# Convolution sums in PSUM, and the seven half products of a group continued in three PSUM banks

## The chip, the cores and the metric

The kernel runs on one core of one Trainium2 chip. The metric is device time in microseconds (us) of one execution; lower is better. "PE" is the tensor engine, "DVE" the vector engine, "ACT" the scalar engine, "POOL" GpSimd and "SP" the queue that issues most transfers. PSUM is the tensor engine's output memory: eight banks of 512 float32 values in each of 128 partitions.

## What is computed

Three blocks, one after the other, on 1024 tokens of 1024 channels in float32. The parts that the change touches are a gated feed-forward network in the first block, the input product, gates, rotary turn and depthwise convolution of the second, and the input product of the third. Cut to that:

```python
# block 1
u_, g_ = (rmsnorm(x) @ ffn_w_in).split                       # 1024 -> 2 x 2816
x = x + (silu(g_) * u_) @ ffn_w_out
# block 2
a, b, cg, q, k, v, gate = (modulated_norm(x) @ w_in_2).split # 1024 -> several x 1024
y = a * sigmoid(b)
y = causal_depthwise_conv(y, conv_w_2, conv_b_2)             # 31 taps per channel
y = silu(layernorm(y)) ...                                   # then a product, times silu(cg)
r = retention(rotary(q), rotary(k), v, silu(gate))           # 4 heads of 256, in chunks of 128 tokens
# block 3
u_s5, z_s5, z_ssd, xBC, dt = (rmsnorm(x) @ w_in_3).split     # 1024 -> ...
```

## The kernel before

Every product of float32 operands is made of three matmuls per tile of weights: both operands are split into a high and a low part (the high part by ACT at L151, the low part by DVE or POOL at L152), and high times high, high times low and low times high are summed in PSUM (L625 to L627 in the class `Mixed`, L226 to L228 elsewhere).

The class `Mixed` (L554 to L672) computes two tiles of 128 outputs for all 1024 tokens, four halves of 128 x 512, with seven products of half matrices in place of eight. One such set is called a group here. A product is 12 matmuls of 128 x 512 (four tiles of weights, three matmuls each), so a group is 84. The parts of the weights are sums and differences of quarters of the weight matrix, made by POOL in place (L597, L599, L602, L605) in the raw tiles that SP loads (L584). The products are run in the order of `ORDER` (L566): a11, a12, s2, s3, s1, s4, a22. Each one goes to a PSUM bank of its own (`WITH`, L568: three banks "mm", two "pa", two "pb"; an eighth, "pc", is for small things), and `gather` (L631) takes it from there: ACT copies a11 (L639), and DVE makes seven additions of 128 x 512, each of a tile in SBUF and the bank (L636), of which s1 needs two. In SBUF the partial sums are carried from one half of the outputs to the next.

`Mixed` is used in four places:

- the feed-forward network's input (`FFN.products`, L728): 22 groups. When a group is complete DVE multiplies both of its output tiles with the row factors (L744, L746), ACT applies Silu, POOL multiplies the two (L747). The low parts of the weights are split by DVE.
- its output (L867 to L900): 8 groups, where ACT, DVE and POOL add the products to the residual `h`; POOL adds what lies in a tile `v` (L865).
- the input of block 2 (`block2`, L1151 to L1246): 24 groups in the order of `plan`: two gates, two convolution pairs, then six times one convolution pair and two of the groups q, k and v, and two gates at the end. Here the low parts are split by POOL (`on_pool`, L1222), except in the first two groups. For q and k, DVE and POOL turn the result (L1201 to L1206: four multiplications by DVE and two additions by POOL for each half of the tokens). For a convolution pair, DVE writes a * sigmoid(b) to the tile `A[c]` (L1192), and 32 steps for its 31 taps are put on a list of background work.
- the input of block 3 (`block3`): 12 groups, behind which POOL runs a scan.

The first two groups of each use are interleaved by `early` (L654), since their second factors come late.

The convolution (`tap`, L1139): per tile of 128 channels one DVE instruction for the first tap (L1143) and 30 for the others (L1147): `acc = A[:, j:j+1024] * w_j + acc`, with 128 x 1024 elements. `acc` lies in SBUF. The last tap writes to `A[c]`. There are eight such tiles, so 8 first taps and 240 others. They are paced by the tensor engine's products: each product of four tiles of weights adds `rate` x 4/16 steps (`worked`, L231), with the rate RT = 6.5, or RQ = 5.5 in the groups q and k; each step may start only behind the last DVE addition of the products (`core.paced`, L1172, used in `tick`, L157). What is left of the taps when the groups are through is run in the next stage, the retention (L1248 to L1428), whose background work at the rate RB is otherwise the layer norm of the convolution (`ln_sum` to `ln_scale`): it needs all taps.

A scheduler orders the instructions of each engine when the kernel is built; on the chip each engine runs its own list strictly in order, and waits where an operand or a place is not ready.

Of the kernel before, what the change touches and what calls it, by code (L numbers as in the profile page):

```python
# [32 lines left out]
RQ = 5.5  # L33
RT = 6.5
# [23 lines left out]
class Core:  # L58
    """Constants, shared pools and the dense products that every part uses."""

    def __init__(self, ctx, tc, ins):
# [11 lines left out]
        self.ps = ctx.enter_context(tc.tile_pool(name="psum", bufs=1, space=PSUM))  # L73
        self.dr = ctx.enter_context(tc.tile_pool(name="dram", bufs=1, space=DRAM))
# [54 lines left out]
    def load_blocks(self, eng, b0, b1):  # L129
        """Blocks of 128 of those vectors."""  # L130
# [41 lines left out]
    def behind(self, steps):  # L172
        """Steps that are to run behind the coming products, whose results wait for them."""
# [6 lines left out]
    def result(self, evac):  # L180
        """A product is emitted: evac() takes it from PSUM, once no step is left."""
# [7 lines left out]
    def norm_steps(self, acc, pool, to, **kw):  # L189
        """Steps to to["rbc"] = rsqrt of the token means of acc, over partitions."""  # L190
# [13 lines left out]
    def weights(self, w, row0, nk, col0, ncol=P, order=lambda t: t, into=None):  # L204
        """Columns col0.. of rows row0.. of w as [128, nk, ncol] parts; order(t) views the parts' columns as w's."""
# [12 lines left out]
    def mm3(self, ps, wts, xs, half, k0=0, start=True, stop=True, ncol=P):  # L218
        """ps[ncol, 512] += weights.T @ x over the k tiles of xs (each [128, 2, 1024])."""
# [11 lines left out]
    def worked(self, n):  # L231
        """Products with n tiles of weights are emitted: a share of the other work may follow."""
# [26 lines left out]
    def rows(self, r, pool):  # L259
        """[128 tokens, n] in two parts"""  # L260
# [6 lines left out]
    def spread_halves(self, rt, tag="pc"):  # L267
        """Parts of [128 tokens, 8] -> for each half, [128, 512] in PSUM, the same in every partition."""
# [9 lines left out]
    def over_partitions(self, rt, pool, tag="rbc", bufs=1, out=None, psum="pc"):  # L278
        """Parts of [128 tokens, 8] -> [128, 1024], the same in every partition."""
# [6 lines left out]
    def square_sum(self, acc, src, sl, first, pool, gain=None, bufs=2):  # L286
        """acc[:, sl] += (src * gain)^2"""
# [9 lines left out]
    def small_transposed(self, src, PT):  # L297
        """Tokens-major DRAM [1024, 256] -> two channel tiles, split."""
# [15 lines left out]
def attention(core, X, scratch):  # L314
    """Stick-breaking attention of every head, its output split in place of X; p @ ple_w_proj goes to DRAM meanwhile."""
# [7 lines left out]
    with ExitStack() as st:  # L323
# [63 lines left out]
        def projections():  # L387
            """Every pair's q, k and v, a few products at a time."""
# [16 lines left out]
            # X is free now  # L405
# [35 lines left out]
        def fill(n, limit):  # L441
            """Emit n (on average) of the products' pieces, but none of the pair after the next."""
# [232 lines left out]
def halves(t):  # L675
    return t[:, hs(0)], t[:, hs(1)]
# [1931 lines left out]
```

## Time and profile before

| what | value |
|---|---|
| median of 3 runs | 3820.76 us (3819.53 to 3821.97) |
| span of the profiled execution | 3820.3 us |
| PE busy | 3470.7 us (91%) |
| DVE busy | 2853.5 us (75%) |
| POOL busy | 1981.7 us (52%) |
| ACT busy | 1479.0 us (39%) |
| taps L1147 into `cacc` | 232, 425.3 us, mean 1833 ns |

The profile is of one execution. "Busy" is the time in which an engine has an instruction in work; matmuls overlap, so a busy PE need not be at its peak. A share over the whole span is an average over stages that are limited by different things, so the rows below are mostly of single stretches of time. Line numbers (L1147) are those of the kernel before. [...]

### The profile page before, as it was taken

The page shows a single profiled execution, that of the slowest core. Times are in us where ns is not written, and L with a number is a line of the kernel's source. Part 1 is how long each engine was busy: PE and PEld are TensorE (multiplying, and loading weights), DVE is VectorE, ACT ScalarE, POOL GpSimd, SP SyncE. Part 2 cuts the span into 40 slices and gives each one's busy share as a digit, 9 for nine tenths or more (in the row PEclk, how much of TensorE's full clock was granted, in tenths as well). Part 3 has the DMA queues.
Part 4 walks back from the last instruction along what each step waited for, and adds up shares of the span by engine and source line. Part 5 has one row for each costly group of instructions (what it writes and reads, how often), then busy time and mean ns, then how long its engine had stood idle before and what let it go on. Part 6 is the DMA issues. An engine that isn't in the chain of part 4 may idle for free. (4 is left out here: it accounts for less than half of the span.)

```text
span 3820.3 us, 45970 instructions
## 1 busy us (share of the span) xinstructions
PE 3470.7 (91%) x16540; PEld 2789.2 (73%) x16540; DVE 2853.5 (75%) x3453; ACT 1479.0 (39%) x2551; POOL 1981.7 (52%) x1690
## 2 busy tenths in 40 slices
PE   8999999999999999877878898989999679899998
PEld 7878777777787787755656677768778468677776
DVE  7888897888878646699999997784768455655644
ACT  5666683422234345311212224223432113753334
POOL 2333342566655434788898744244518874331122
PEclk9999999999999999999989999999999889899999
DMA  4111026333336324212211344466453125225513
GB/s 140 37 35 31 27 83 235 98 111 113 103 104 199 97 90 139 72 50 72 61 64 53 111 143 133 114 196 194 144 155 111 57 75 157 87 75 177 193 48 113
DMA packets 431134, 409.85 MB, mean 107 GB/s; under 512 B 34059, under 2 KB 364347, under 8 KB 430907
## 3 DMA queue, kind: packets, MB, share of 16 engines
q1 hardware_dynamic: 396164, 330.27, 27.8%
q0 software_dynamic: 21088, 68.19, 4.9%
q10 hardware_dynamic: 13655, 8.46, 0.8%
q8 instruction: 131, 2.15, 0.2%
q14 instruction: 96, 0.79, 0.1%
HBM read 284.80 MB, written 122.03 MB: 106 GB/s over the span
## 5 line engine op out<-in xcount | busy, mean ns | idle before, releaser
L151 ACT ACTIVATE whi<-raw 128x512 fp32r<-128x512 f32 (+3 forms) x610 | 431.3, 736 | 1105.7 <-POOL raw L599 234.1
L152 DVE TENSOR_TENSOR wlo<-raw,whi 128x512 fp32r<-128x512 f32 (+3 forms) x456 | 517.7, 1154 | 136.4 <-ACT whi L151 134.1
L226 PE MATMUL mm<-x,whi 128*128 128x512 f32 x1152 | 462.2, 402 | 6.1 <-DVE h L830 2.8
L227 PE MATMUL mm<-x,whi 128*128 128x512 f32 x1152 | 460.5, 400 | 3.5 <-DVE x L152 3.3
L228 PE MATMUL mm<-x,wlo 128*128 128x512 f32 x1152 | 458.7, 399 | 3.2 <-DVE wlo L152 3.2
L1147 DVE SCALAR_TENSOR_TENSOR cacc<-cv,par,cacc 128x1024 f32<-128x1024 f32 x232 | 425.3, 1833 | 2.5
L485 POOL TENSOR_TENSOR s<-s,f 128x127 f32<-128x127 f32 (+1 forms) x192 | 194.0, 1018 | 293.3 <-DVE f L484 189.2
L152 POOL TENSOR_TENSOR wlo<-raw,whi 128x512 fp32r<-128x512 f32 x154 | 296.0, 1941 | 14.9 <-ACT whi L151 14.9
L226 PE MATMUL mm<-yc,whi 128*128 128x512 f32 (+1 forms) x656 | 268.1, 409 | 32.9 <-ACT yc L151 28.2
L227 PE MATMUL mm<-yc,whi 128*128 128x512 f32 (+1 forms) x656 | 267.9, 408 | 4.4 <-DVE yc L152 4.3
L228 PE MATMUL mm<-yc,wlo 128*128 128x512 f32 (+1 forms) x656 | 264.7, 405 | 0.1
L226 PEld LDWEIGHTS mm<-x,whi 128*128 128x128 f32 x1152 | 219.4, 191 | 53.3 <-DVE h L830 3.5
L228 PEld LDWEIGHTS mm<-x,wlo 128*128 128x128 f32 x1152 | 219.3, 190 | 50.1 <-DVE wlo L152 4.7
L227 PEld LDWEIGHTS mm<-x,whi 128*128 128x128 f32 x1152 | 219.6, 191 | 48.8 <-DVE x L152 4.0
L484 DVE TENSOR_TENSOR_SCAN f<-f 128x128 f32<-128x128 f32 (+1 forms) x192 | 195.9, 1034 | 40.2 <-ACT f L477 39.0
L627 PE MATMUL mm<-x,wlo 128*128 128x512 f32 x456 | 186.3, 409 | 30.4 <-POOL wlo L152 17.1
L597 POOL TENSOR_TENSOR raw<-raw 128x512 f32<-128x512 f32 x58 | 91.3, 1574 | 221.6 <-DMA raw<-in_w_in_dram 80.4
L625 PE MATMUL mm<-x,whi 128*128 128x512 f32 x456 | 184.7, 405 | 5.2 <-ACT whi L151 3.8
L627 PE MATMUL pb<-x,wlo 128*128 128x512 f32 x432 | 176.5, 409 | 13.0 <-POOL wlo L152 9.9
L626 PE MATMUL mm<-x,whi 128*128 128x512 f32 x456 | 184.6, 405 | 3.6 <-DVE x L152 3.6
L626 PE MATMUL pb<-x,whi 128*128 128x512 f32 x432 | 174.8, 405 | 4.7 <-DVE x L152 4.7
L625 PE MATMUL pb<-x,whi 128*128 128x512 f32 x432 | 175.7, 407 | 3.5 <-DVE g L636 3.5
(618 smaller groups left out, 9092.4 us busy)
## 6 DMA issues: line engine op xcount, KB each, us to landing
raw<-in_w_in_dram SPq DMA_DIRECT2D x96, 512.0 KB
raw<-in_ffn_w_in_dram SPq DMA_DIRECT2D x44, 512.0 KB
raw<-in_w_out_dram SPq DMA_DIRECT2D x32, 512.0 KB
g<-g_dram SPq DMA_DIRECT2D x56, 256.0 KB
raw<-in_sb_w_in_dram SPq DMA_DIRECT2D x24, 512.0 KB
raw<-in_ada_w_dram SPq DMA_DIRECT2D x24, 512.0 KB
raw<-h_dram SPq DMA_DIRECT2D x18, 512.0 KB
g_dram<-t POOLq DMA_DIRECT2D x8, 1024.0 KB, 5.2
```

What stands on the lines that cost most here:

```text
L151: nc.scalar.activation(hi, src, AF.Copy)
L152: return (eng or nc.vector).tensor_tensor(lo, src, hi.bitcast(F32), ALU.subtract).ins
L226: nc.tensor.matmul(ps, w_h, x[:, 0, sl], start=start and k == 0, stop=False)
L227: nc.tensor.matmul(ps, w_h, x[:, 1, sl], start=False, stop=False)
L228: self.last = nc.tensor.matmul(ps, w_l, x[:, 0, sl], start=False, stop=stop and k == n - 1).ins
L484: nc.vector.tensor_tensor_scan(rev, rev, rev, 1.0, ALU.mult, ALU.bypass)
L485: nc.gpsimd.tensor_tensor(s[:, :m - 1], s[:, :m - 1], f[:, 1:m], ALU.mult)
L597: self.eng.tensor_tensor(at["s1"], at["a21"], at["a22"], ALU.add)
L625: nc.tensor.matmul(ps, hi[:, i], x[i][:, 0], start=i == 0, stop=False)
L626: nc.tensor.matmul(ps, hi[:, i], x[i][:, 1], start=False, stop=False)
L627: self.core.last = nc.tensor.matmul(ps, lo[:, i], x[i][:, 0], start=False, stop=i == self.N - 1).ins
L1147: nc.vector.scalar_tensor_tensor(out, A[c][:, j:j + S], core.vec("conv_w_2", j * KT + c), state["acc"], ALU.mult, ALU.add)
```

## The change

Two things are changed, and the pacing is fitted to them.

1. The convolution's running sum `acc` is a PSUM tile of two banks instead of an SBUF tile. The three banks "mm" are given back for the time of block 2's groups (`core.banks`), and taken again after it. The taps' rates are RT = 8 and RQ = 6, and what is left of the taps is run before the stage ends.
2. The products of a group go to three banks, a, b and c, and continue there: bank a takes a11, then s2, then s3, then a22 on top of each other; bank b takes a12; bank c takes s1, then s4. Between them ACT copies the partial sum out (after a11, s2 and s1), and DVE adds the bank to a tile three times (after a12, s3 and s4). The last value of bank a is taken by ACT (with the gate's or the convolution's function, where there is one) or, in the feed-forward network, by a DVE multiplication with the row factors. The order is a11, a12, s2, s1, s3, s4, a22. So a group has 3 DVE additions for 7, and 3 copies by ACT, and a fourth at its end in blocks 2 and 3, for 1.

The diff, cut to its core:

```diff
-RQ = 5.5
-RT = 6.5
+RQ = 6
+RT = 8
...
+        self.lent = ctx.enter_context(ExitStack())
+        self.banks()
...
+    def banks(self, name="psum_mm"):
+        self.lent.close()
+        self.psm = self.lent.enter_context(self.tc.tile_pool(name=name, bufs=1, space=PSUM))
+
     def psum(self, tag, shape=(P, HALF)):
-        bufs = {"mm": 3, "pa": 2, "pb": 2, "pc": 1}[tag]
-        return self.ps.tile(list(shape), F32, tag=tag, name=self.nm(tag), bufs=bufs)
+        pool, bufs = {"mm": (self.psm, 3), "acc": (self.psm, 1), "pa": (self.ps, 2), "pb": (self.ps, 2), "pc": (self.ps, 1)}[tag]
+        return pool.tile(list(shape), F32, tag=tag, name=self.nm(tag), bufs=bufs)
...
 class Mixed:
-    ORDER = ("a11", "a12", "s2", "s3", "s1", "s4", "a22")
-    WITH = {"a11": ("11", "mm"), "a12": ("21", "pb"), "s2": ("t2", "pa"), "s3": ("t3", "mm"), "s1": ("t1", "pb"),
-            "s4": ("22", "pa"), "a22": ("t4", "mm")}
+    ORDER = ("a11", "a12", "s2", "s1", "s3", "s4", "a22")
+    WITH = {"a11": ("11", "a"), "a12": ("21", "b"), "s2": ("t2", "a"), "s1": ("t1", "c"), "s3": ("t3", "a"),
+            "s4": ("22", "c"), "a22": ("t4", "a")}
+    TAGS = {"a": "pb", "b": "pa", "c": "pa"}
...
     def product(self, grp, name, x):
-        which, tag = self.WITH[name]
-        ps, x = self.core.psum(tag), x[which]
+        which, bank = self.WITH[name]
+        x, first = x[which], name in ("a11", "a12", "s1")
+        if first:
+            grp["ps"][bank] = self.core.psum(self.TAGS[bank])
+        ps, more = grp["ps"][bank], not first
         for i in range(self.N):
-            nc.tensor.matmul(ps, hi[:, i], x[i][:, 0], start=i == 0, stop=False)
+            nc.tensor.matmul(ps, hi[:, i], x[i][:, 0], start=first and i == 0, stop=False, skip_group_check=more)
...
-    def gather(self, name, ps, y):
+    def gather(self, name, ps, y, last):
         if name == "a11":
+            nc.scalar.activation(g1, ps, AF.Copy)
+        elif name == "a12":
+            add(g1)
+        elif name == "s2":
             nc.scalar.activation(g2, ps, AF.Copy)
-        elif name == "a12":
-            add(g1, g2)
-        elif name == "s2":
-            add(g2, g2)
+        elif name == "s1":
+            nc.scalar.activation(u2, ps, AF.Copy)
         elif name == "s3":
-            add(u1, g2)
-        elif name == "s1":
-            add(u2, u1)
-            add(g2, g2)
+            add(u2)
         elif name == "s4":
-            add(g2, g2)
+            add(g2)
         else:
-            add(u1, u1)
+            last(u1, ps)
...
     def early(self, product, gather, step=lambda: None):
         both(0, "a11", "a12")
         step()
-        product(0, "s1")
+        both(0, "s1")
         product(0, "s4")
         step()
         both(1, "a11", "a12")
         step()
         both(0, "s2", "s3")
-        gather(0, "s1")
         gather(0, "s4")
         both(0, "a22")
-        both(1, "s2", "s3", "s1", "s4", "a22")
+        both(1, *self.ORDER[2:])
...
 (FFN.products)
+            def scaled(u1, ps):
+                nc.vector.tensor_tensor(u1, ps, norm["rbc"][:, hs(0)], ALU.mult)
...
-                nc.vector.tensor_tensor(u, u, rbc, ALU.mult)
+                nc.vector.tensor_tensor(u[:, hs(1)], u[:, hs(1)], rbc[:, hs(1)], ALU.mult)
...
 (the FFN's output in block1)
+                        out = {"a11": g1, "a12": g1, "s2": g2, "s1": u2, "s3": u2, "s4": g2, "a22": u1}[name]
+                        if name in ("a11", "s2", "s3"):
+                            v = gp.tile([P, HALF], F32, tag="v", name=core.nm("v"), bufs=2)
                             nc.scalar.activation(v, ps, AF.Copy)
+                            add(out, v, nc.gpsimd)
                         elif name == "s1":
+                            v = gp.tile([P, HALF], F32, tag="v", name=core.nm("v"), bufs=2)
+                            nc.scalar.activation(v, ps, AF.Copy)
+                            add(out, v, nc.gpsimd)
                         else:
-                            add(u1, ps)
+                            add(out, ps)
...
 (block2)
-                    state["acc"] = cvp.tile([P, S], F32, tag="cacc", name=core.nm("cacc"))
+                    state["acc"] = core.psum("acc", (P, S))
...
         core.rate = RT
+        core.banks("psum_conv")
...
+                of = {"gate": AF.Silu, "conv": AF.Sigmoid}.get(kind, AF.Copy)
+                           lambda u1, ps: nc.scalar.activation(u1, ps, of))
-                if name != "a11":
+                if name in ("a12", "s3", "s4"):
                     core.paced = mix.last
...
-                if name in ("a11", "a12", "s2", "s3"):
+                if name in ("a11", "a12", "s1", "s2", "s3"):
                     gather(f, name)
...
             while turns:
                 turns.pop(0)()
+            core.paced = None
+            core.drain()
         scratch["mixed"].close()
+        core.banks()
```

The last group of block 2 (L1231) keeps its order a11, a12, s1, s4, s2, s3, a22. In block 3 the last value of bank a is copied by ACT. Comments and docstrings were taken out as well.

## Rows read from the trace of the kernel before

**Rows 1.** The page, busy time of each engine over the whole span.
```profile
PE 3470.7 (91%) x16540; PEld 2789.2 (73%) x16540; DVE 2853.5 (75%) x3453; ACT 1479.0 (39%) x2551; POOL 1981.7 (52%) x1690
```
**Rows 2.** Busy us and instructions per engine by stretch, then clock, DMA share, GB/s.
```profile
700.00:1160.00 460.00, 443.62 (x1911) 357.13 (x1909) 386.57 (x401) 151.07 (x242) 284.34 (x186) 0.99 0.32 103
1160.00:1335.00 175.00, 166.77 (x706) 133.57 (x706) 130.59 (x166) 66.18 (x113) 92.50 (x63) 0.98 0.45 145
1600.00:2187.00 587.00, 475.50 (x1853) 360.34 (x1852) 578.58 (x434) 118.75 (x197) 512.57 (x261) 0.92 0.21 64
2187.00:2395.00 208.00, 185.11 (x927) 155.52 (x926) 173.24 (x245) 79.91 (x122) 96.10 (x90) 0.96 0.45 142
2700.00:2975.00 275.00, 266.37 (x1313) 211.55 (x1312) 208.46 (x247) 95.80 (x138) 146.16 (x199) 0.98 0.41 130
```
**Rows 3.** What PE waited for in 1600 to 2187: total us, times, longest.
```profile
PE mm L627 <- POOL wlo L152: 48.1, 27, 5.8
PE pa L627 <- POOL wlo L152: 23.4, 13, 4.2
PE pa L625 <- ACT whi L151: 13.2, 5, 6.0
```
**Rows 4.** Instructions of single lines, whole span: ns min/median/max, first to last start.
```profile
L1147 DVE SCALAR_TENSOR_TENSOR cacc<-cv,par,cacc x232: 1249/1720/3467, 1601.5 to 2278.2; 128x1024 f32<-128x1024 f32 x116
L636 DVE TENSOR_TENSOR g<-g,pb x116: 671/675/707, 729.3 to 2969.8; 128x512 f32<-128x512 f32 x116
L1205 DVE TENSOR_TENSOR u<-u,cos x16: 680/1771/1784, 1676.0 to 2109.6; 128x512 f32<-128x512 f32 x16
L152 DVE TENSOR_TENSOR x<-h,x x16: 675/678/1780, 1505.8 to 1541.4; 128x512 fp32r<-128x512 f32 x16
L152 POOL TENSOR_TENSOR wlo<-raw,whi x154: 1269/2244/2283, 1569.9 to 2163.2; 128x512 fp32r<-128x512 f32 x154
L639 ACT ACTIVATE g<-mm x58: 576/582/677, 727.5 to 2960.3; 128x512 f32<-128x512 f32 x58
```
**Rows 5.** DVE in order of time (start, us), while POOL computes nothing.
```profile
2205.81 5.24 DVE L1147 SCALAR_TENSOR_TENSOR cacc<-cv,par,cacc 128x1024 f32<-128x1024 f32 x4
```
**Rows 6.** Groups of DVE instructions in 1600 to 2187: busy us, mean ns, idle before.
```profile
L1147 DVE SCALAR_TENSOR_TENSOR cacc<-cv,par,cacc 128x1024 f32<-128x1024 f32 x190 | 362.8, 1910 | 2.1
L636 DVE TENSOR_TENSOR g<-g,pb 128x512 f32<-128x512 f32 x42 | 28.2, 674 | 0.6 <-ACT g L639 0.6
...
L1205 DVE TENSOR_TENSOR u<-u,cos 128x512 f32<-128x512 f32 x16 | 26.7, 1667 | 0.0
...
L1201 DVE TENSOR_TENSOR rt<-g,sin 128x512 f32<-128x512 f32 x16 | 22.7, 1418 | 3.6 <-POOL g L1204 3.6
...
L1192 DVE TENSOR_TENSOR cv<-g,u 128x1024 f32<-128x1024 f32 x7 | 13.4, 1915 | 0.0
...
L1143 DVE TENSOR_SCALAR cacc<-cv,par 128x1024 f32<-128x1024 f32 x7 | 8.1, 1164 | 0.1
```
**Rows 7.** PE in order of time (start, us) in block 2's groups, undisturbed.
```profile
1657.16 0.39 PE L627 MATMUL mm<-t,wlo 128*128 128x512 f32 x1
...
1658.56 0.39 PE L627 MATMUL mm<-t,wlo 128*128 128x512 f32 x1
```
**Rows 8.** Groups of POOL instructions in 1600 to 2187.
```profile
L152 POOL TENSOR_TENSOR wlo<-raw,whi 128x512 fp32r<-128x512 f32 x144 | 283.3, 1986 | 7.1 <-ACT whi L151 7.1
...
L597 POOL TENSOR_TENSOR raw<-raw 128x512 f32<-128x512 f32 x20 | 34.8, 1741 | 38.1 <-DMA raw<-in_w_in_dram 33.6 <-PE pa L626 4.5
```
**Rows 9.** Taps in 2190 to 2450: a group of DVE instructions.
```profile
L1147 DVE SCALAR_TENSOR_TENSOR cacc<-cv,par,cacc 128x1024 f32<-128x1024 f32 x42 | 62.5, 1489 | 0.4
```
**Rows 10.** What PE waited for in 2187 to 2395, the retention.
```profile
PE pc L1376 <- DVE rstate L1385: 10.7, 2, 9.6
```
**Rows 11.** What PE waited for in 700 to 1160, the feed-forward network's input.
```profile
PE mm L627 <- DVE wlo L152: 5.9, 5, 1.9
...
PE mm L625 <- ACT g L639: 1.0, 1, 1.0
```

More of the change, by code (lines that the diff above doesn't have):

```diff
@@ L575, in group @@
     def group(self, w, row0, ca, cb, order=lambda t: t):
-        return {"src": (w, row0, ca, cb), "raw": {}, "ready": {}, "order": order}
+        return {"src": (w, row0, ca, cb), "raw": {}, "ready": {}, "order": order, "ps": {}}
     def load(self, grp, which):
@@ L621, in product, with add @@
         hi, lo = grp["ready"].get(name) or self.part(grp, name)
-        which, tag = self.WITH[name]
-        ps, x = self.core.psum(tag), x[which]
+        which, bank = self.WITH[name]
[3 more added lines that the diff above has]
+        ps, more = grp["ps"][bank], not first
         for i in range(self.N):
-            nc.tensor.matmul(ps, hi[:, i], x[i][:, 0], start=i == 0, stop=False)
-            nc.tensor.matmul(ps, hi[:, i], x[i][:, 1], start=False, stop=False)
-            self.core.last = nc.tensor.matmul(ps, lo[:, i], x[i][:, 0], start=False, stop=i == self.N - 1).ins
+            nc.tensor.matmul(ps, hi[:, i], x[i][:, 0], start=first and i == 0, stop=False, skip_group_check=more)
+            nc.tensor.matmul(ps, hi[:, i], x[i][:, 1], start=False, stop=False, skip_group_check=more)
+            self.core.last = nc.tensor.matmul(ps, lo[:, i], x[i][:, 0], start=False, stop=i == self.N - 1, skip_group_check=more).ins
         self.core.worked(self.N)
         return ps
-    def gather(self, name, ps, y):
+    def gather(self, name, ps, y, last):
         nc = self.core.nc
         (g1, g2), (u1, u2) = y
-        def add(out, a):
-            self.last = nc.vector.tensor_tensor(out, a, ps, ALU.add).ins
+        def add(out):
+            self.last = nc.vector.tensor_tensor(out, out, ps, ALU.add).ins
         if name == "a11":
+            nc.scalar.activation(g1, ps, AF.Copy)
+        elif name == "a12":
+            add(g1)
+        elif name == "s2":
             nc.scalar.activation(g2, ps, AF.Copy)
-        elif name == "a12":
-            add(g1, g2)
-        elif name == "s2":
-            add(g2, g2)
+        elif name == "s1":
+            nc.scalar.activation(u2, ps, AF.Copy)
         elif name == "s3":
-            add(u1, g2)
-        elif name == "s1":
-            add(u2, u1)
-            add(g2, g2)
+            add(u2)
         elif name == "s4":
-            add(g2, g2)
+            add(g2)
         else:
-            add(u1, u1)
+            last(u1, ps)
     def early(self, product, gather, step=lambda: None):
@@ L847, in block1 @@
             x11, x21, t1, x22 = (ffn.x[n] for n in ("11", "21", "t1", "22"))
-            places = [(y3, x11, x21, y0, y1, t1, x22), (y2, y3, x11, x21, y0, y1, t1)]
+            places = [(y3, x11, x21, y0, t1, y1, x22), (y2, y3, x11, x21, y0, t1, y1)]
             def second(chunk, name, pool):
@@ L1183, in gather, with gate @@
                         turns.pop(0)()
-            def gate(i, k, y):
-                nc.scalar.activation(y, y, AF.Silu)
+            def gate(i, k, y, rest):
+                nc.scalar.activation(y[:, rest], y[:, rest], AF.Silu)
                 nc.sync.dma_start(heads["gate"][i, :, k], y)
@@ L1190, in conv @@
                 nc.vector.memset(A[c][:, :PAD], 0.0)
-                nc.scalar.activation(b, b, AF.Sigmoid)
+                nc.scalar.activation(b[:, hs(1)], b[:, hs(1)], AF.Sigmoid)
                 nc.vector.tensor_tensor(A[c][:, PAD:], a, b, ALU.mult)
@@ L1242, in block2 @@
                         core.split(t1[:, 0], t1[:, 1], a)
-            for name in ("s1", "s4", "a22"):
+            for name in ("s4", "a22"):
                 gather(f, name)
@@ L1921, in gather @@
                 at[f, "g"] = gp.tile([P, S], F32, tag="g", name=core.nm("g"), bufs=2)
-            if name == "s3":
+            if name == "s1":
                 at[f, "u"] = gp.tile([P, S], F32, tag="u", name=core.nm("u"))
             g, u = at[f, "g"], at.get((f, "u"))
-            mix.gather(name, at[f, name], (halves(g), halves(u) if u is not None else (None, None)))
+            mix.gather(name, at[f, name], (halves(g), halves(u) if u is not None else (None, None)),
+                       lambda u1, ps: nc.scalar.activation(u1, ps, AF.Copy))
             out, m = (u_out, 2 * f) if f < 4 else (z_out, 2 * (f - 4))
```

28 lines of the change are left out of this document (6 added, 22 removed).

## The prediction

> **What bounds the kernel now.** I read the busy times over the whole span first [rows 1]: PE 91%, which says "tensor bound" and hides that the stages differ. So next the busy times by stage [rows 2]. In the feed-forward network's input and output (700 to 1335) and in block 3's groups (2700 to 2975) PE is busy 96, 95 and 97%: what they could gain is at most their idle 16 + 8 + 9 us. In block 2's groups, from the first tap to the last product (1600 to 2187, 587 us), it is another engine: DVE is busy 578.6 of 587 us, POOL 513, PE only 476, at a granted clock of 0.92. Then the waits there [rows 3]: PE waits for POOL's low parts of the weights. So DVE and POOL are both full, and the reader should ask whether they fill each other.
>
> They do [rows 4, 5]. Four taps with no POOL instruction beside them take 5.24 us, 1.31 each; in the stage the mean is 1.91 [rows 6]. A rotary multiplication of 512 elements takes 0.68 us at best and 1.77 in the median; POOL's split 1.27 at best, 2.24 in the median. Both grow by about 1 us, the length of the other's instruction: of DVE's instructions with two tile inputs in SBUF and POOL's, one waits for the other. The additions L636, with one input in SBUF and one in PSUM, run in the same minutes and took 671 to 707 ns in all 116 cases: they never wait. So a tap with its sum in PSUM, which reads one tile from SBUF, should drop out of this contest.
>
> **The change part by part.**
>
> *The taps.* In the stretch there are 196 taps now (190, and 6 that write the tile `cv`) at 1.91 us, 374 us. The counts of steps: the list gets 8 x 32 = 256; with rates 8 and 6 a product adds 2 or 1.5 steps, so a group of seven 14 or 10.5. From the fourth group on that is 13 x 14 + 8 x 10.5 = 266, and adding up group by group the list never runs dry before the last group and is empty by that group's second product. So all 240 taps come into this stage, and nothing is left to the drain. One costs 1.31 (the undisturbed row). No row shows DVE writing to PSUM: from below I take 1.25, the shortest tap, from above 1.91, today's mean, and choose 1.31, since the addition that reads PSUM costs the same 675 ns as a split between SBUF tiles [rows 4]. 240 x 1.31 = 314, so 60 us less for 44 taps more. The 8 first taps go from 1.16 to perhaps 1.3 each: 2 us more.
>
> [...]
>
> *The additions.* Per group 7 become 3. The stretch has 21 groups: 147 - 63 = 84 additions x 0.674 = 57 us less DVE. ACT gets 3 more copies of 0.58 us per group [rows 4], 37 us on top of 119 of 587: it lies beside. If ACT were held up by a split that waits for POOL, it would not; that is rival C.
>
> *The rotary multiplications.* 64 at a mean of 1.50 (the two rows stand for four), 96 us. POOL is left with the same 261 instructions, but with 1.27 instead of 1.97 us for most; their chance to meet falls. Bounds 0.68 and 1.50; I take 1.3: 13 us less. The seven products a * sigmoid(b) (1.9 us [rows 6]), also with two inputs in SBUF, are left as they are.
>
> *Sum for the stage.* DVE 578.6 - 60 + 2 - 57 - 13 = 451 us. What is late next: PE, at 1853 matmuls x 0.233 us (six starts in 1.40 us [rows 7]; the few short ones counted as full) = 432; POOL, 261 x 1.27 = 331 plus about 45 for the DVE instructions that still hold it up, plus its waits for loads, 34 now [rows 8]. DVE stays the fullest, but no longer alone. With PE at nine tenths I give DVE 35 us of waiting where it had 8: 486 us, **101 less**. Bounds: no shorter than PE allows (about 450), no longer than today's 587 as long as taps cost under 1.8.
>
> *The retention.* It loses the 44 taps, some 65 us (62.5 in [rows 9], and two last taps), and the layer norm can start at once. DVE is busy 173 of 208 us there, PE idle 23, of which the longest wait, 9.6 of 10.7 us, is for a DVE instruction [rows 10]. The burst of the layer norm's own work stays. Between 0 and 23 less; I take **10 less**.
>
> *Direct continuations.* In `early`, s3 follows s2 and a22 follows s3 in the same bank with no product between; at three of the four uses that is 6 places. In block 2's last group s4 follows s1, s3 s2, a22 s3: 3 more. PE waits there for its last matmul to leave (0.39 [rows 7]) and then a copy of 0.58 or an addition of 0.68: about 1.1 us. 9 x 1.1 = **10 more**.
>
> *All other groups.* Each has four places where PE needs a bank emptied, and one product between (12 x 0.233 = 2.8 us) as cover: the copies take 0.58, the addition 0.68. While DVE or ACT runs late by more than 2.1 us, PE stands, with all its later products queued behind. Bank a has two buffers and b and c share two, so nothing else is nearer. The nearest row: today's copy held PE up for 1.0 us in all of the feed-forward network's input [rows 11]; over some 20 copies that is 0.05 each, and 0.05 x 168 places (42 groups) 8 us. On the other side DVE loses 4 additions per group, in the feed-forward network 3 and half of a multiplication, and its late splits cost PE 5.9 us there in the largest row; all that can be won is the 33 us of idle of the first paragraph. I set this to zero, bounds -33 and +8. The moved product s1 brings its split and its u tile one place forward; its raw tile is loaded for s2 already, so no transfer and no SP place moves. In the network's output POOL has four additions per group as now.
>
> Total, made against the profiled span of 3820.3, half a microsecond under the median: 3820.3 - 101 - 10 + 10 = **3719 us**.
>
> **The rivals.**
>
> *B, the tap doesn't get cheaper.* If writing and reading the same PSUM banks slows DVE, or a tap still contends with POOL, the stage carries 44 more taps at the old price: 451 + 240 x 0.6 + 13 + 8 = 616, 29 more, 3849 us, **slower**. It decides from a tap of 1.79 us on. For it: no row shows a DVE write to PSUM. Against it: 116 additions of [rows 4] without one wait.
>
> *C, the continuations hold PE up in the stages that PE bounds.* 22 + 8 + 12 groups with 4 places each are 168. At 0.5 us each, 84 us, 3803; from 0.60 us on all is lost, and it is slower. For it: engines run in order, and in block 2 ACT waits for POOL before its splits; DVE is busy 84% in the network's input. Against it: 2.8 us of cover, the wait of 1.0 us in [rows 11], and DVE's smaller load.
>
> *D, PE becomes the bound in block 2.* If taps cost 1.25 and the rotary multiplications run nearly free, DVE needs 410 us and PE's 432 decide; with 18 of idle 450, 137 less: 3683. Against it: q and k groups carry 10.5 taps and 8 multiplications, some 26 us of DVE for 19.6 of PE, and the two do not even out.
>
> *E, tight coupling.* Three engines at 80 to 95% with few buffers lose 80 us in place of 35: 3764.
>
> *That it does not do what it says*: taps left for the drain would stand alone before the retention, 1.31 us each. The count above leaves 10 steps to spare, 13 us at most.
>
> **How the numbers follow.** Forecast 3719 (3695 to 3745): 0.58. D 0.14, E 0.10, C 0.12, B 0.06. The range that should hold it 8 times in 10 takes in D and E and the milder half of C: 3675 to 3790. About 0.2%, 8 us, is what a measurement of this kernel can tell from no change. Faster: forecast, D, E and half of C, 0.88; within 0.2%: 0.03; slower, B and the heavier C: 0.09.
>
> **What would show it.** Right: taps with a mean of 1.25 to 1.4 us and a narrow spread; none after the last group; POOL's split near 1.3 to 1.6; the stage near 486 us with DVE still the fullest and the granted clock above 0.92; the feed-forward stages as long as before. Wrong: taps above 1.8 us (B); waits of PE's first matmul of s2, s3, s4 or a22 for ACT copies or DVE additions of some hundred ns each all over the network's stages (C); PE over 95% busy in block 2 (D).

## The result and the profile after

The changed kernel takes 3765.47 us (median of four runs, 3763.95 to 3770.01) beside 3820.15 of the kernel before on the same chip: a ratio of 0.9855, 95% interval 0.9843 to 0.9867. It is 1.4% faster, by 55 us where 101 were forecast. The profiled execution has a span of 3762.0 us, 58 less than that of before. In the rows below the line numbers are those of the changed kernel: tap L1153 (first tap L1149), addition L650, the copies L653 (a11), L657 (s2) and L659 (s1), split L159 and L160, matmuls of a group L638 to L640, rotary multiplications L1210 to L1214.

The busy times by stage, with the columns of [rows 2] and its first four stages in the same order (feed-forward input, its output, block 2's groups from the first tap to the last product, the retention from its first matmul):

```profile
700.00:1182.00 482.00, 447.19 (x1890) 353.86 (x1888) 355.66 (x336) 173.26 (x286) 259.17 (x184) 0.98 0.31 99
1182.00:1355.00 173.00, 158.96 (x666) 126.38 (x667) 104.50 (x125) 72.83 (x129) 90.67 (x63) 0.98 0.44 139
1636.00:2125.00 489.00, 441.79 (x1833) 348.26 (x1832) 442.60 (x395) 149.56 (x260) 360.11 (x260) 0.95 0.24 74
2135.00:2318.00 183.00, 172.58 (x889) 146.93 (x888) 105.73 (x192) 77.95 (x116) 82.21 (x82) 0.96 0.50 156
```

The third window ends, like that of [rows 2], when DVE is through with the last group, 10 us before the retention's first matmul; the last matmul of a group itself ended at 2168 before and ends at 2123 now. Block 2's groups went from 587 to 489 us. DVE fell from 578.6 to 442.6 us there, and no engine is full any more: DVE is busy 91% of it and PE 90%. The network's input went the other way: about the same matmuls (1911 in 460 us before, 1890 in 482 now), DVE less busy, and PE idle for 35 us where it was 16.

The groups of DVE instructions in 1636 to 2125 (busy us, mean ns, idle before), beside [rows 6]:

```profile
L1153 DVE SCALAR_TENSOR_TENSOR acc<-cv,par,acc 128x1024 f32<-128x1024 f32 x232 | 298.1, 1285 | 4.3
L650 DVE TENSOR_TENSOR g<-g,pa 128x512 f32<-128x512 f32 x41 | 27.9, 682 | 20.2 <-PE pa L640 17.2 <-issue 2.8
L1210 DVE TENSOR_TENSOR rt<-g,sin 128x512 f32<-128x512 f32 x16 | 21.9, 1366 | 3.8 <-DMA v_dram<-rt 2.5 <-POOL g L1213 1.3
...
L1214 DVE TENSOR_TENSOR u<-u,cos 128x512 f32<-128x512 f32 x16 | 13.7, 857 | 0.0
...
L1149 DVE TENSOR_SCALAR acc<-cv,par 128x1024 f32<-128x1024 f32 x8 | 10.7, 1343 | 0.2
```

And the taps over the whole span (ns min/median/max, first and last start), beside [rows 4]:

```profile
L1153 DVE SCALAR_TENSOR_TENSOR acc<-cv,par,acc x232: 1273/1289/1293, 1636.9 to 2109.8; 128x1024 f32<-128x1024 f32 x116
```

A tap takes 1.285 us where the mean was 1.91, and the spread is gone: 1273 to 1293 where it was 1249 to 3467. The last one starts at 2109.8, ahead of the last product. What PE waits for, in block 2's groups (first three lines, beside [rows 3]) and in the network's input (the last four, beside [rows 11]):

```profile
PE pb L640 <- POOL wlo L160: 27.4, 16, 5.0
PE pa L638 <- ACT u L659: 12.9, 5, 5.6
PE pb L638 <- ACT whi L159: 6.2, 7, 2.1
```
```profile
PE pb L638 <- DVE u L650: 6.3, 6, 2.4
PE pb L638 <- ACT g L657: 6.3, 7, 4.5
...
PE pc L283 <- DVE rrow L271: 2.8, 1, 2.8
...
PE pa L638 <- ACT u L659: 2.2, 1, 2.2
```

In both there is a new kind: the first matmul of a continuation (L638) waits for the copy or the addition that empties its bank.

To see where the 46 missing us went (43 between the two profiled executions), I cut each profiled execution at two events: the first tap, and the end of the last matmul of block 2's output product.

| kernel | start to first tap | to the end of block 2's output | to the end | span |
|---|---|---|---|---|
| before | 1600 | 1100 | 1120 | 3820 |
| after | 1636 | 996 | 1130 | 3762 |
| after - before | +36 | -104 | +10 | -58 |

So block 2 gave 104, and the two other parts, in which PE is the busiest engine (95% and 90% of them before), took 46 back. The experiments ask three things: what in block 2 gave the 104, what the 36 are, and whether something new now bounds block 2.

### The profile page after: what moved, and what is told of

It is laid out like the page before. It is cut to its first block, busy times and chain, and to the rows that moved or that the text cites. A ratio compares the mean times of both kernels' runs of the same rounds, so it can differ in the third digit from the quotient of the medians.

```text
span 3762.0 us, 45800 instructions
## 1 busy us (share of the span) xinstructions
PE 3450.0 (92%) x16540; PEld 2777.5 (74%) x16540; DVE 2562.5 (68%) x3211; ACT 1568.7 (42%) x2729; POOL 1801.3 (48%) x1690
## 4 chain that ended last, share of the span: by engine, by line
PE 58%; DVE 13%; POOL 11%; DMA 8%; issue 6%; ACT 4%; SPq 0%; ACTq 0%; POOLq 0%; DVEq 0%
PE mm L234 9%; PE mm L236 9%; PE mm L235 9%; PE pb L640 4%; PE pb L638 4%; PE pb L639 4%; DVE wlo L160 3%; PE pa L638 3%; PE pa L640 3%; PE pa L639 3%; POOL sc L1863 2%; POOL s_H L1865 2%; POOL s_H L1864 2%; POOL wlo L160 2%; ACT whi L159 1%
## 5 line engine op out<-in xcount | busy, mean ns | idle before, releaser
L159 ACT ACTIVATE whi<-raw 128x512 fp32r<-128x512 f32 (+3 forms) x610 | 430.9, 736 | 791.2 <-PE pb L639 216.8
L160 DVE TENSOR_TENSOR wlo<-raw,whi 128x512 fp32r<-128x512 f32 (+3 forms) x456 | 551.2, 1231 | 218.4 <-ACT whi L159 214.8
L234 PE MATMUL mm<-x,whi 128*128 128x512 f32 x1152 | 463.1, 403 | 9.3 <-ACT whi L159 4.4
L236 PE MATMUL mm<-x,wlo 128*128 128x512 f32 x1152 | 458.7, 399 | 6.0 <-DVE wlo L160 6.0
L235 PE MATMUL mm<-x,whi 128*128 128x512 f32 x1152 | 461.6, 401 | 0.5 <-DVE x L163 0.3
L1153 DVE SCALAR_TENSOR_TENSOR acc<-cv,par,acc 128x1024 f32<-128x1024 f32 x232 | 298.1, 1285 | 4.3
L638 PE MATMUL pa<-x,whi 128*128 128x512 f32 x648 | 261.5, 404 | 22.5 <-ACT u L659 15.1
L640 PE MATMUL pa<-x,wlo 128*128 128x512 f32 x648 | 260.0, 402 | 11.3 <-DVE wlo L160 11.1
L639 PE MATMUL pa<-x,whi 128*128 128x512 f32 x648 | 259.4, 400 | 7.5 <-DVE x L160 7.5
L640 PE MATMUL pb<-x,wlo 128*128 128x512 f32 x576 | 233.3, 410 | 31.2 <-POOL wlo L160 22.5
L638 PE MATMUL pb<-x,whi 128*128 128x512 f32 x576 | 236.6, 411 | 26.3 <-ACT whi L159 8.8
L160 POOL TENSOR_TENSOR wlo<-raw,whi 128x512 fp32r<-128x512 f32 x154 | 215.9, 1421 | 80.6 <-ACT whi L159 80.5
L639 PE MATMUL pb<-x,whi 128*128 128x512 f32 x576 | 233.2, 405 | 3.1 <-DVE x L160 3.1
L607 POOL TENSOR_TENSOR raw<-raw 128x512 f32<-128x512 f32 x58 | 80.0, 1379 | 246.8 <-DMA raw<-in_ffn_w_in_dram 120.9
```

The costliest lines, as they stand in the source:

```text
L159: nc.scalar.activation(hi, src, AF.Copy)
L160: return (eng or nc.vector).tensor_tensor(lo, src, hi.bitcast(F32), ALU.subtract).ins
L234: nc.tensor.matmul(ps, w_h, x[:, 0, sl], start=start and k == 0, stop=False)
L235: nc.tensor.matmul(ps, w_h, x[:, 1, sl], start=False, stop=False)
L236: self.last = nc.tensor.matmul(ps, w_l, x[:, 0, sl], start=False, stop=stop and k == n - 1).ins
L607: self.eng.tensor_tensor(at["s1"], at["a21"], at["a22"], ALU.add)
```

## Experiments

Each kernel is the changed kernel ("after") or the kernel before with a small edit; the same cut follows for all of them at the end.

**The feed-forward network's input as before.** `FFN` gets the class of before, with seven banks and seven additions; the rest is the changed kernel.

```diff
-        self.mix = Mixed(core, sm)
+        self.mix = MixedOld(core, sm)     # products, gather and early of the kernel before
```

> The changed kernel, but the feed-forward network's input (22 groups) has its products in banks of their own and the seven additions again; its output, blocks 2 and 3 stay changed. Theory (the loss of 21 us there comes from the continued banks): the input's stretch falls from 482 to about 460 us, the whole to about 3744 us. Rival (the loss is from another order or place of tiles that comes with the new pools): no more than 5 us gained, about 3762 us.

Measured: 3735.38 us, ratio 0.9779 (0.9764 to 0.9793), 30 us under the changed kernel. The first tap comes at 1611 instead of 1636: 25 of them lie in the network's input. The class carries the banks, the order of the products and the copies together, so this run does not tell these apart.

**Its output as before too.**

> As e1, and the feed-forward network's output (8 groups) has the old products and additions too. Theory (input and output together lost 33 us to the continued banks): about 3732 us, 12 less than e1. Rival (not the banks): about 3760 us.

Measured: 3728.73 us, ratio 0.9755 (0.9739 to 0.9771). The first tap is at 1601, where it was before the change. So the changed products cost the network 35 us: 25 in the input, 10 in the output. Put on the 30 groups with four places each, that is 0.29 us a place. What the trace of the changed kernel itself books on copies and additions in the input is less: the 14.8 us of the three rows above (6.3, 6.3 and 2.2), 0.17 a place. This is rival C, at a little over half the price that I gave it or less, and in the stages where it was expected.

**The order of the products held on PE.** In the changed kernel the scheduler may put matmuls of two products in turn on PE. This is what it does to a continuation, in order of time (start, us; in brackets the idle time before and what ended it):

```profile
893.52 0.40 PE L638 MATMUL pa<-x,whi 128*128 128x512 f32 x1
...
893.76 0.40 PE L638 MATMUL pb<-x,whi 128*128 128x512 f32 x1
...
896.33 0.39 PE L640 MATMUL pb<-x,wlo 128*128 128x512 f32 x1
...
896.56 0.39 PE L639 MATMUL pa<-x,whi 128*128 128x512 f32 x1
...
896.75 0.60 ACT L657 ACTIVATE g<-pb 128x512 f32<-128x512 f32 x1 [2.70 <-PE pb L640]
896.79 0.40 PE L640 MATMUL pa<-x,wlo 128*128 128x512 f32 x1
...
897.41 0.50 PE L638 MATMUL pb<-x,whi 128*128 128x512 f32 x1 [0.22 <-ACT g L657]
```

Bank pb's s2 ends, ACT copies it, and s3 is to continue in pb. Of the twelve matmuls of s1 that should lie between them only two are left: the other ten were run earlier, ahead of all twelve of s2 (the last of the ten at 893.52, the first of s2 at 893.76). The cover of 2.8 us that I counted on is half a microsecond here. In the next kernel each product of the network may be issued only behind the last matmul of the product ahead of it:

```diff
+        if self.strict and self.core.last is not None:
+            with self.core.tc.issue_after(self.core.last):
+                all_of()                  # the product's 12 matmuls
+        else:
+            all_of()
```

In the order as built, continuations of the input with less than four matmuls between fall from 12 of 88 to 3.

> The changed kernel, and in the feed-forward network (input and output) the tensor engine's order is held: the first matmul of a product stands behind the last of the product before, so that the next product is whole between two parts of one bank. In the changed kernel's list 12 of the 88 continuations of the network's input have fewer than 4 matmuls between the two parts, here 3. Theory (the cover was lost in the order): the 15 us of waits for copies and additions in the input fall to 6 or less, the whole to about 3752 us. Rival (copies and additions come late however the products are ordered, or the order was needed to wait for weights): these waits stay, or waits for weights take their place, 3765 us or more.

Measured: 3753.37 us, ratio 0.9823 (0.9802 to 0.9845); 12 less than the changed kernel, the first tap at 1620. Its four runs go from 3748.69 to 3765.20, and its interval just touches that of the changed kernel (0.9843 to 0.9867), so the 12 us are likely rather than sure. About a third of the network's loss is then cover that the order of the matmuls took away. In 700 to 1170 the waits on copies and additions fall from 14.8 us to 9.5, not to the 6 that I expected:

```profile
PE pb L642 <- DVE wlo L160: 8.1, 7, 1.3
PE pc L283 <- DVE rrow L271: 5.4, 1, 5.4
PE pb L640 <- ACT g L664: 3.0, 2, 2.3
PE pc L283 <- DVE rrow L272: 2.4, 1, 2.4
PE pb L640 <- ACT g L660: 2.3, 1, 2.3
```

Two rows of 2.2 and 2.0 us make up the 9.5. Beside them stand the low parts of the weights (8.1 us; 7.0 in the changed kernel) and the norm factors of the start, which PE waits for at the first groups (before the change this kind of wait had one row there, 0.6 us).

**The convolution sum back in SBUF.** The changed kernel, with `acc` in the SBUF tile of before. It separates the additions from the place of the taps: DVE keeps its 84 additions less.

```diff
-                    state["acc"] = core.psum("acc", (P, S))
+                    state["acc"] = cvp.tile([P, S], F32, tag="cacc", name=core.nm("cacc"))
```

> The changed kernel with the convolution's running sum back in SBUF; the continued banks, the rates and the order stay. Theory (taps in PSUM are spared the contest with POOL): taps at 1.8 to 1.9 us again, block 2's groups at 590 to 620 us in place of 489, the whole at 3865 to 3895 us, slower than the kernel before. Rival (the gain of block 2 comes from the fewer additions): at most 40 us over the changed kernel, under 3805 us.

Measured: 3907.0 us, ratio 1.0225 (1.0205 to 1.0246): 142 slower than the changed kernel, 85 slower than before, and 12 over the upper end of what I expected. From the first tap to the retention (1636 to 2294), the window, DVE's taps, POOL's splits and PE's longest wait:

```profile
1636.00:2294.00 658.00, 498.58 (x1879) 382.06 (x1878) 624.26 (x397) 149.83 (x262) 533.80 (x265) 0.87 0.19 59
```
```profile
L1153 DVE SCALAR_TENSOR_TENSOR cacc<-cv,par,cacc 128x1024 f32<-128x1024 f32 x232 | 443.9, 1913 | 4.4
```
```profile
L160 POOL TENSOR_TENSOR wlo<-raw,whi 128x512 fp32r<-128x512 f32 x143 | 291.9, 2060 | 55.8 <-ACT whi L159 55.8
```
```profile
PE pb L640 <- POOL wlo L160: 103.1, 24, 12.7
```

The taps are at 1.91 us again, and POOL's split goes from 1.43 us in the changed kernel to 2.06: the two fill each other, as [rows 4 to 6] said, and one operand moved to PSUM undoes it for the taps and most of it for POOL (1.27 at best [rows 4]). In the kernel before, the order of time shows one waiting for the other (start, us; the lines are those of the kernel before):

```profile
1673.80 2.30 DVE L1147 SCALAR_TENSOR_TENSOR cacc<-cv,par,cacc 128x1024 f32<-128x1024 f32 x1
...
1674.98 2.27 POOL L1204 TENSOR_TENSOR g<-g,rt 128x512 f32<-128x512 f32 x1
...
1676.03 1.77 DVE L1205 TENSOR_TENSOR u<-u,cos 128x512 f32<-128x512 f32 x1
...
1677.21 1.71 POOL L152 TENSOR_TENSOR wlo<-raw,whi 128x512 fp32r<-128x512 f32 x1
```

POOL's addition ends 1.15 us behind the tap in which it starts, the rotary multiplication 0.55 behind that addition, the split 1.12 behind the multiplication. In 1600 to 2187 it goes like this almost everywhere: of 218 POOL instructions that start during a tap or a rotary multiplication 213 end 1.12 to 1.16 us behind it; of those that start during a POOL instruction, 52 of 54 rotary multiplications end 0.54 or 0.55 us behind it and 154 of 164 taps 1.08 to 1.10. With the sum in PSUM a tap takes 1.285 us and the split 1.43. Rates, order and banks are the same on both sides, so the 142 us are the price of the sum's place alone, beside the continued banks.

**The taps alone.** The kernel before with the sum in PSUM, the new rates and the drain, and one bank "mm" left in block 2; the seven products keep banks of their own and all seven additions stay.

```diff
-RQ = 5.5
-RT = 6.5
+RQ = 6
+RT = 8
...
-                    state["acc"] = cvp.tile([P, S], F32, tag="cacc", name=core.nm("cacc"))
+                    state["acc"] = core.psum("acc", (P, S))
...
+        core.banks("psum_conv", 1)        # "mm" keeps one bank
```

> The kernel before with the convolution's running sum in PSUM and the new rates alone; the products keep their banks (but one bank mm in place of three in block 2) and their seven additions. Theory: taps at 1.29 us; DVE's work in block 2's groups 443 + 84 x 0.67 = 499 us, the stage 515 to 545 us, no loss in the feed-forward network: 3755 to 3775 us in all, about as fast as the whole change. Rival (fewer additions carry the gain, or the single bank mm holds PE up): 3795 us or more.

Measured: 3733.68 us, ratio 0.9772 (0.9758 to 0.9787), better than either theory expected and 32 us better than the whole change. From the first tap to the retention (1596 to 2084), and, for the same stretch of the changed kernel, the second line:

```profile
1596.00:2084.00 488.00, 431.17 (x1814) 337.51 (x1812) 461.88 (x462) 121.12 (x199) 373.74 (x267) 0.96 0.25 77
```
```profile
1636.00:2135.00 499.00, 451.79 (x1877) 356.54 (x1876) 443.40 (x396) 151.12 (x262) 365.89 (x266) 0.95 0.25 77
```

DVE runs 66 instructions more (84 additions more, 18 taps less), and the stretch is no longer. So the additions taken from DVE did not shorten these groups, as long as u has one tile (the next experiments). Part of their price shows later: the 18 taps, 23 us, run on in the retention, and over the whole of block 2 the kernel needs 1009 us, where the changed one with the old network needs 991. The new rates without the move to PSUM were not run, so what they give by themselves is open.

**A second u tile.** In block 2 the copy of s1 (L659) writes the tile u, of which there is one. In a group of q or k it still holds the group before, turned and on its way to DRAM. The changed kernel, in order of time:

```profile
1801.48 1.28 DVE L1153 SCALAR_TENSOR_TENSOR acc<-cv,par,acc 128x1024 f32<-128x1024 f32 x1
...
1802.67 0.81 DVE L1214 TENSOR_TENSOR u<-u,cos 128x512 f32<-128x512 f32 x1
1802.90 1.71 POOL L607 TENSOR_TENSOR raw<-raw 128x512 f32<-128x512 f32 x1
...
1804.57 1.25 POOL L1215 TENSOR_TENSOR u<-u,rt 128x512 f32<-128x512 f32 x1
...
1805.86 0.34 SPq L1217 DMA_DIRECT2D q_dram<-u  x1
1806.13 0.60 ACT L653 ACTIVATE g<-pb 128x512 f32<-128x512 f32 x1 [10.98 <-DMA q_dram<-g]
...
1808.55 0.60 ACT L659 ACTIVATE u<-pa 128x512 f32<-128x512 f32 x1 [1.82 <-DMA q_dram<-u]
...
1809.20 0.80 PE L638 MATMUL pa<-x,whi 128*128 128x512 f32 x1 [5.59 <-ACT u L659]
...
1810.22 0.63 PE L640 MATMUL pa<-x,wlo 128*128 128x512 f32 x1
```

The chain is: rotary multiplication behind a tap on DVE, POOL's addition behind a sum of weights, SP's store of u, ACT's copy, which waits for the store to land, and PE's first matmul of s4, which continues in the bank that ACT is to copy. PE stands for 5.59 us. For the first 2.5 of them another store held ACT: the copy of the next group's a11, ahead in ACT's list, had waited 10.98 us for the store of g and began at 1806.13. Then PE is slow: from 1809.2 on the matmuls start 0.43 us apart where they start 0.23 apart undisturbed. Two windows just after, at a lower and at a higher granted clock:

```profile
1809.20:1813.20 4.00, 4.00 (x9) 3.17 (x10) 3.91 (x4) 0.63 (x1) 0.00 (x0) 0.50 0.00 0
1813.60:1818.00 4.40, 4.40 (x21) 3.55 (x20) 3.69 (x4) 2.27 (x4) 3.23 (x3) 1.00 0.00 0
```

Nine matmuls in 4 us at a granted clock of 0.50 (a share of the tensor engine's full clock), 21 in 4.4 us at 1.00. ACT's copy of s1 waits for such stores seven times, 15.8 us in all, with the splits of the next products queued behind it:

```profile
ACT u L659 <- DMA q_dram<-u: 8.3, 3, 5.9
ACT u L659 <- DMA k_dram<-u: 7.5, 4, 4.0
```

Moving the sum to PSUM left room in SBUF for a second tile:

```diff
-                    at[f, "u"] = tp.tile([P, S], F32, tag="u", name=core.nm("u"), bufs=1)
+                    at[f, "u"] = tp.tile([P, S], F32, tag="u", name=core.nm("u"), bufs=2)
```

> The changed kernel with two buffers in place of one for the tile u in block 2. Theory (the copy of s1 to u, which now comes two products earlier than the first write to u did, waits for the store of the group before, and PE behind it for 12.9 us): that wait goes, the stage from the first tap to the retention falls from 499 to about 488 us, the whole to about 3755 us. Rival (PE waits for POOL's low parts instead): within 4 us of 3765.

Measured: 3723.34 us (3715.96 to 3730.88), ratio 0.974 (0.9719 to 0.9761), 42 less than the changed kernel, four times what I expected. From the first tap to the retention, and PE's waits there:

```profile
1632.00:2073.00 441.00, 413.99 (x1801) 334.25 (x1800) 422.51 (x385) 149.80 (x259) 375.54 (x265) 0.98 0.27 85
```
```profile
PE pa L1367 <- DMA k<-k_dram: 11.7, 1, 11.7
PE pb L638 <- DVE u L650: 6.3, 4, 4.0
PE pb L640 <- POOL wlo L160: 6.3, 3, 3.1
```

The 58 us between 499 and 441 have three parts. 76 matmuls of other work (1877 - 1801) now run after it: 76 x 0.233 = 18 us, which the retention gives back. PE's idle time falls from 47 to 27 us. And a matmul takes 0.230 us instead of 0.241 (busy over count), 20 us over 1801 of them, with a granted clock of 0.98 for 0.95. So the waits themselves are 20 us, and as much again went with them in the time of the matmuls, which the higher clock shows; I had counted the waits only. Of the waits, those for the stores (12.9 us) are gone, and those for POOL's low parts fall from 27.4 us to 9.0 (the 6.3 above and 2.7), since ACT's splits were queued behind its copies. No copy of ACT waits for a store any more, that to g included: the scheduler orders the lists anew for two tiles, so the 42 us are what the tile gives together with that order. One reason in the expectation is wrong: the first write to u does not come earlier than it did. In both kernels it stands behind a group's fourth product, s3 before and s1 now. The longest wait, 11.7 us, is new: the first matmuls of the retention stand for the load of k.

**The second u tile with the old network, and with the taps alone.**

> e2 (old products in the feed-forward network, continued banks in blocks 2 and 3, taps in PSUM) with two buffers for u in block 2. Theory: 10 us under e2, about 3718 us. Rival: 3725 to 3730 us.

Measured: 3700.05 us (3691.34 to 3704.32), ratio 0.9683 (0.9666 to 0.97). 29 less than without the second tile, where I expected 10.

> e4 (the kernel before with the taps in PSUM alone) with two buffers for u in block 2. In e4 DVE's write to u waits 9 us for stores, and PE 16 us for that addition. Theory: 8 to 12 us under e4, about 3724 us. Rival (other waits take over): 3730 to 3736 us. Beside e7 it tells what the continued banks are worth in blocks 2 and 3.

Measured: 3716.33 us, ratio 0.9723 (0.9708 to 0.9738), 17 less than without, where I expected 8 to 12. With an addition by DVE as the first writer of u, the wait for the stores is shorter (8.9 us of DVE's in block 2's groups, 15.8 of ACT's in the changed kernel); PE waited 15.8 us for these additions. Now the fewer additions show in the groups as well: from the first tap to the retention's first matmul this kernel takes 456 us, the one before it, with continued banks, 440. Whether a second tile would have helped the kernel before was not tried: its sum takes the place in SBUF. Its trace has no row with DVE waiting for these stores in 1600 to 2187.

**Continued banks in block 2 alone.** The kernel with the old network and two u tiles, and block 3's groups as before too.

```diff
-        mix = Mixed(core, tp)
+        mix = MixedOld(core, tp)          # block 3
...
-            if name == "s1":
+            if name == "s3":
```

> The kernel with the feed-forward network of the kernel before and two u tiles in block 2, and block 3's twelve groups also computed as before: seven products in banks of their own, seven additions. The continued banks are left in block 2 alone. Theory: in stages that PE bounds, a continued bank costs 0.2 to 0.3 us per place (33 us over 30 groups in the feed-forward network); twelve groups of block 3 with four places each are 48 places, so 7 to 14 us come back, and the time is 3686 to 3693 (3700.05 with them). Rival: the network's loss came from its own ends (norm factors late at its start, additions on POOL in its output), not from the continuations; block 3 then gains nothing, 3697 to 3703.

Measured: 3689.14 us (five runs, 3686.72 to 3698.91), ratio 0.9663 (0.965 to 0.9676): 11 less in the median, inside the range of the theory. But the runs of the two kernels overlap (3691.34 to 3704.32 with continued banks in block 3), and so do the intervals, so the difference leans to the theory and is not clear of noise. This kernel has the lowest median of all, 131 us under the kernel before and 76 under the changed one.

The cut at the two events, for all of them:

| kernel | groups in the network | taps | block 2, block 3 | u | to first tap | block 2 | rest | span |
|---|---|---|---|---|---|---|---|---|
| before | old | SBUF | old, old | 1 | 1600 | 1100 | 1120 | 3820 |
| after | new | PSUM | new, new | 1 | 1636 | 996 | 1130 | 3762 |
| input old | old, new | PSUM | new, new | 1 | 1611 | 990 | 1128 | 3729 |
| network old | old | PSUM | new, new | 1 | 1601 | 991 | 1135 | 3727 |
| order held | new | PSUM | new, new | 1 | 1620 | 1000 | 1132 | 3752 |
| sum in SBUF | new | SBUF | new, new | 1 | 1636 | 1148 | 1126 | 3910 |
| taps alone | old | PSUM | old, old | 1 | 1596 | 1009 | 1126 | 3731 |
| second u | new | PSUM | new, new | 2 | 1632 | 956 | 1126 | 3714 |
| network old, second u | old | PSUM | new, new | 2 | 1600 | 961 | 1129 | 3690 |
| taps alone, second u | old | PSUM | old, old | 2 | 1596 | 997 | 1121 | 3714 |
| block 2 alone, second u | old | PSUM | new, old | 2 | 1599 | 964 | 1122 | 3685 |

Each row is one execution; those of "second u" and "network old, second u" are 7 and 9 us under the median of their kernels, so a few us of a cell are chance. Read down a column, each part has its price. The network: 36 us for the changed products. Block 2: 91 us for the taps in PSUM with their rates (1100 to 1009; beside continued banks, with the rates alike, 152: 1148 to 996), 18 for the continued banks there (1009 to 991), and 36 of them once u has two tiles (997 to 961). The rest: 1120 to 1126 with block 3 as before (four kernels, mean 1122), 1126 to 1135 with continued banks (seven, mean 1129): 7 us over 48 places, 0.15 each, with single rows up to 5 us from their mean.

## Why the prediction was right in its direction and wrong in its size

**The taps: right.** 240 x 1.285 = 308 us where 314 stood; no tap was left for the drain. The choice between 1.25 and 1.91 by the price of an addition that reads PSUM held within 2%: the taps that read and write PSUM took 1285 ns, the undisturbed ones in SBUF 1310 [rows 5]. Rival B falls with it. Taken alone the taps bring 91 us in block 2, with what follows from them: my sum without the additions leaves DVE 578.6 - 60 + 2 - 13 = 508 us in the stage, and in the kernel with the taps alone it is 461.9 and the 23 of the taps that run later, 485.

**The rotary multiplications: right.** The four lines sum to 73.6 us for 64, 1.15 each where 1.3 stood: 9 us better. Those of L1210, with a mean of 1366 ns, still contend.

**The stage: right in its number, wrong in its reason.** 489 us measured, 486 forecast; DVE 442.6, forecast 451. But the sum was one of DVE's busy time plus 35 of waiting, and in it the additions counted 57 us. The kernel with the taps alone keeps all additions and takes 488 us to the retention, where the changed one takes 499 and the one before took 597. DVE's busy time no longer set the end. As the runs stand, some 90 of the 104 us in block 2 come from the taps with their rates and 13 from the continued banks.

**The u tile: this step failed.** "The moved product s1 brings its split and its u tile one place forward ... no transfer and no SP place moves" I costed at nothing, looking at loads only. The first write to u did not even move: it stands behind the fourth product in both kernels. What changed is who writes. u's place is freed by a store, behind a tap, POOL and SP; the first writer of u was DVE, and became ACT, with PE waiting directly behind it for the same bank. With a second tile the kernel is 42 us faster. It was a new bound of block 2, and rival E ("tight coupling") is what it looks like from outside. That block 2 met its forecast all the same is luck, two errors of opposite sign: the taps brought more than their term, the additions less. It is luck too that the total, 3765, is the 3764 of E: E put its loss into block 2, whose groups took 489 us and not 531, and the loss lies in the stages before and behind.

**All other groups at zero, bounds -33 and +8: this step failed, and it is what the total missed.** The network lost 36 us and block 3 about 7, 43 over 168 places, 0.26 each if all of it is put on the places. My bound took the one old row in which a copy held PE up, 1.0 us in all [rows 11]. In the kernel before that copy freed a bank of a ring; in the changed one the very next user of the same bank waits for it, so the row was no bound for it: the rows of this kind sum to 14.8 us in the network's input. And the cover of 2.8 us supposed the order of the products as written in the code; the scheduler runs the matmuls of two products in turn, and holding the order gave some 12 of the 36 us back, which is not clear of noise. Some 7 us more are waits for the norm factors at the first groups (2.8 in the row above, 2.4 and 1.8 in two more), 0.6 before; block 3 has 4.9 us of the same kind, where it had 1.4. That the new order of `early` brought them was not tested, and how the rest of the 36 us divides stays open. The 33 us that PE's idle time could give were not to be had: DVE's lower load freed nothing there.

**Retention and direct continuations: small.** The stage from its first matmul is 183 us where it was 198, but 9 of these 15 us come back in the products behind it, which carry work moved out of it: to the end of block 2 the stretch behind the groups is 6 us shorter (-104 and +98), 10 forecast. The direct continuations are 12 and not 9: in `early` s4 follows s1 in bank c as well, once at each of the three uses. In the network's first group PE waited 0.7 us at s3 and 0.8 at a22, where 1.1 stood, and 2.2 at s4, with matmuls of the norm factors between; the others were not measured by themselves.

Of the ten us that the last part lost, 7 are block 3's groups by the means of the rows; the rest is within the spread of single rows.

## What to carry to other kernels

Where DVE and POOL both work from SBUF and slow each other down, move one tensor operand of DVE's longest instruction to PSUM first: here that one line, with rates fitted to it, was worth some 90 us, and the larger rewrite around it gave less in its stage and cost time in the others. A bank that is read out and then continued ties the tensor engine to another engine's queue at every place; here such a place cost 0.15 us in block 3 and up to 0.29 in the network, where late norm factors and lost cover are in the price. Look in the order as built, not in the code, for what lies between. When a tile gets a new first writer, look up what its last reader was, a store included, and which engine now waits for it.

## What the runs showed of the hardware

A DVE instruction whose sum is read from and written to PSUM ran at 1273 to 1293 ns in all 232 cases, beside a POOL that is 74% busy; with the sum in SBUF, the same instruction had a mean of 1913 ns. The first tap, which only writes to PSUM, takes 1336 to 1347 ns; in the kernel before, into SBUF, the same instruction took 801 to 1715 ns, 990 in the median. In the median it was the shorter one there.

One wait of PE went on costing when it was over: behind the 5.6 us of it shown above, nine matmuls took 4 us at a granted clock of 0.50, where 21 take 4.4 us at 1.00, so 2.1 us more. Over block 2's groups 20 us less of idle time went with 20 us less in the time of the matmuls, from 0.241 to 0.230 us each, at a granted clock of 0.98 for 0.95.
